# Gate products of the recurrence on half the rows of TensorE, and the decay squared on ScalarE, in a hybrid decoder layer

## The chip, the cores and the metric

One core of a Trainium2 chip runs the whole layer as one program. The metric is the device time of one execution in microseconds (us). A profiled execution also has a span, from its first to its last instruction. The engines are TensorE (PE, its weight loads shown as PEld), VectorE (DVE), ScalarE (ACT), GpSimd (POOL) and SyncE (SP), which issues the DMAs here. A time of any table or row is counted from the start of the span.

## What is computed

The layer normalises x, projects it by w_in, runs a recurrence (RG-LRU) on 512 channels beside latent attention with 8 heads, joins both through w_out, and ends with a SwiGLU FFN and a gated per-layer embedding. 1024 positions, width 1024, all in float32. The change lies in the recurrence, whose two gates r and i are block-diagonal products: 8 blocks of 64 channels, each with a 64x64 matrix of its own.

```python
xc = causal_depthwise_conv(x_rnn, conv_w, conv_b)
xb = xc.reshape(B, S, RNN_BLOCKS, RNN_BW)          # 8 blocks of 64
r = sigmoid(einsum('bsnc,ncd->bsnd', xb, w_a) + b_a).reshape(B, S, D_RNN)
i = sigmoid(einsum('bsnc,ncd->bsnd', xb, w_x) + b_x).reshape(B, S, D_RNN)
log_a = -LRU_C * r * softplus(-lru_L)
a = exp(log_a)
mult = sqrt(-expm1(2.0 * log_a))
bterm = mult * (i * xc)
_, h = associative_scan(_lin_rec_combine, (a, bterm), axis=1)
return h * gelu(x_gate)
```

## The kernel before

All activations lie transposed: channels on the 128 partitions, the 1024 positions along the row, worked in two halves of 512 (`HS`). Each float32 product is made of three products of rounded parts (fp32r): high weights with the high and the low part of the data, and low weights with the high part (names ending in `_h` and `_l`). Function `mm` issues these three for both halves, each half into a PSUM bank of its own. PSUM is handed out as four single banks (`bank`) and two double ones (`wide`). The banks of a pair are named `_a` and `_b`, by `pair`.

The stages follow each other: the latent and key projection (`g1`), then ten column tiles of w_in (`wn`: two latent query tiles, four tiles r0 to r3 of the recurrence, four gate tiles g0 to g3), of which one half goes into pairs of banks (`wn_a`, `wn_b`) and the other into wide ones (`wn`). For a tile r the convolution makes `xc` and its two parts (`rg_front`, L794). After two such tiles `rg_pair` (L802) is put in: per tile and gate a 128x128 weight matrix whose diagonal holds the two 64x64 blocks and which is zero elsewhere (`_layout`, L1529 to L1534), six products into `rg_a` and `rg_b` (the two halves of the positions), and two sigmoids of 128x512 that read the banks (L813). Then the decay: `rg_t` by Tanh, `rg_r` by Exp, its square on VectorE into `xc` (L822), the root of the term before the input, and the scan. Among this work stand the keys (`kr`, `kps`), the values (`v`), the queries (`qps`), then eight heads of scores (`s`), transposes (`tp`) and weighted sums (`av`), the output projection (`wo`), and the FFN, whose products (`ff_z`, `ff_y`, `ff_x`) are made by Strassen-Winograd's scheme with seven products in place of eight.

The order of all of this is not the order of the code. Every call is recorded in a `Plan` (L141) as an operation with a cost and with what it depends on. `Plan.order` (L244) then plays a clock: at each step it looks for each engine through the operations that are ready, takes the one with the lowest key for which its PSUM banks and SBUF slots are free (L289), charges the cost that `cost` (L167) gives it, and moves on. POOL operations, and VectorE operations with two inputs in SBUF or a fast copy form, are marked as using a shared port (`shares`, L197); one that is taken while the port is in use starts when it comes free (L318 to L320), and its engine stands until then. ScalarE's activation tables count 1.28 us a switch. All instructions are recorded in one helper, so that every row of the profile has the line of `emit` (L372), and instructions are told apart by their tiles. `emit` issues them in the planned order, each engine in its own sequence.

Of the kernel before, what the change touches and what calls it, by code (L numbers as in the profile page):

```python
# [16 lines left out]
P = 128  # L17
S = 1024
D = 1024
HB = 512  # L20
# [120 lines left out]
class Plan:  # L141
# [25 lines left out]
    def cost(self, eng, fn, a, k, out):  # L167
        w = out.width() if isinstance(out, View) else 0
        if fn == "dma_start":
            v = k["out"] if isinstance(k["out"], View) else k["in_"]  # L170
            return v.shape[0] * v.width() * 4 / 360e3, 2.1
        if eng == "tensor":
            if fn == "transpose":
                return 0.108, 0.18
            return max(w * 0.000417 + 0.0135, 0.113), 0.18
        if eng == "vector":
            if fn == "reciprocal":
                return 0.065 + w * 0.0063, 0.13
            if fn == "tensor_tensor_scan":
                return 0.068 + w * 0.0021, 0.13  # L180
            if fn in ("tensor_reduce", "reduce_sum"):
                return 0.065 + k["in_"].width() * 0.00104, 0.13
            ptr = 0.061 * any(isinstance(x, View) for x in (k.get("scalar"), *a[2:])) if fn == "scalar_tensor_tensor" else 0.0
            one = fn in ("tensor_copy", "tensor_scalar", "tensor_scalar_mul", "tensor_scalar_add", "tensor_scalar_max")
            if one and all(v.buf.tag not in PS for v in [*a, *k.values()] if isinstance(v, View)):
                return 0.068 + w * 0.00052, 0.13
            return 0.068 + ptr + w * 0.00104, 0.13
        if eng == "scalar":
            src = k["in_"] if "in_" in k else a[1]
            c = (0.052 if src.buf.tag in PS else 0.093) + w * 0.000833  # L190
            c += 0.093 * sum(isinstance(k.get(n), View) for n in ("scale", "bias"))
            c += 0.2 * isinstance(k.get("accum_out"), View)
            return c, 0.14
        return 0.15 + w * (0.0033 if fn == "tensor_copy" else 0.0022), 0.14
# [49 lines left out]
    def order(self):  # L244
# [28 lines left out]
        while left:  # L273
            while frees and frees[0][0] <= t:
                _, _, tag, n = heapq.heappop(frees)
                free[tag] += n
            moved = False
            for e in names:
                while future[e] and future[e][0][0] <= t:
                    _, i, o = heapq.heappop(future[e])  # L280
                    heapq.heappush(avail[e], (o.key, i, o))
                if busy[e] > t or not avail[e]:
                    continue
                pick, skipped, best = None, [], None
                tries = 0
                while avail[e] and tries < 40:
                    i, _, o = heapq.heappop(avail[e])
                    tries += 1
                    ok = all(b.placed or free[b.tag] > min(unplaced(b), RES.get(b.tag, 99)) for b in o.bufs)  # L289
                    if ok:  # L290
                        key = i
                        if e == "scalar" and o.table and o.table not in SAME.get(table, ()):
                            key = i + SWITCH
                        if best is None or key < best[0]:
                            if best is not None:
                                skipped.append((best[1], best[2].idx, best[2]))
                            best = (key, i, o)
                        else:
                            skipped.append((i, o.idx, o))
                        if e != "scalar" or key == i:  # L300
                            break
                    else:
                        skipped.append((i, o.idx, o))
                for s in skipped:
                    heapq.heappush(avail[e], s)
                if best is None:
                    continue

                soon = next((r for r, _, x in future[e][:6] if r < t + HOLD and r + 0.05 < t + best[2].cost
                             and x.cost < 0.25 and x.key + 20 < best[0]), None) if e != "tensor" else None  # L310
                if soon is not None:
                    heapq.heappush(avail[e], (best[1], best[2].idx, best[2]))
                    continue
                o = best[2]
                moved = True
                start = t
                c = o.cost
                if o.port:  # L318
                    start = max(t, port)
                    port = start + c  # L320
                if o.table and o.table not in SAME.get(table, ()):
                    table = FIRST[o.table]
                    c += 1.28
                for b in o.bufs:
                    if b.placed:
                        continue
                    b.placed = True
                    free[b.tag] -= 1
                    q, d = queue[b.tag], ahead[b.tag]
                    d[b.pos] = True  # L330
                    while head[b.tag] < len(q) and d[head[b.tag]]:
                        head[b.tag] += 1
                busy[e] = start + c
                o.end = start + c + o.lat
                o.st = start
                out.append((t, o.idx, o))
                left -= 1
                for b in o.bufs:
                    b.left -= 1
                    b.done = max(getattr(b, "done", 0.0), start + c + LAT[e, "tensor"] if b.tag in PS and e != "tensor" else o.end)  # L340
                    if not b.left:
                        heapq.heappush(frees, (b.done, b.pos, b.tag, 1))
                for s in o.succ:
                    s.npred -= 1
                    r = start + c + (LAT[e, s.eng] if (e, s.eng) in LAT else o.lat)
                    s.ready = max(s.ready, r)
                    if not s.npred:
                        heapq.heappush(future[s.eng], (s.ready, s.idx, s))
            nxt = [busy[e] for e in names if busy[e] > t and (avail[e] or future[e])]
            nxt += [future[e][0][0] for e in names if future[e] and future[e][0][0] > t]  # L350
            if frees:
                nxt.append(frees[0][0])
            nxt = [x for x in nxt if x > t]
            if not left:
                break
            if not nxt:
                raise RuntimeError("the plan does not fit")
            t = min(nxt)
# [21 lines left out]
XLATE = 100  # L380
HOLD = 0.15
KLATE = 100
WARM = 9
NV0 = 4
TL = 300
# [14 lines left out]
def hybrid_layer(ctx, tc, xT, pT, pos, vec, const, const2, w1, wn, wrg, wq, wkv, wo, wg, wu, *rest):  # L400
# [114 lines left out]


    order = [(("w1", k), w1[k], 192) for k in range(8)] + [(("wn", i), wn[i], S) for i in range(2)]
    order += [(("rg", 0), wrg, S)] + [(("wn", i), wn[i], S) for i in range(2, 10)]
    order += [(("wkv", 0), wkv, S), (("wq", 0), wq[0], S)]
    order += [(("wq", 1), wq[1], S)]  # L520
    order += [(("wo", n), wo[n], S) for n in NO]
# [280 lines left out]
    def rg_pair(js):  # L802
        yield
        gs = {}
        for j in js:
            xc, x2 = fronts[j]
            r, i = slot("rg_r"), slot("rg_i")
            for t, (dst, b) in enumerate(((r, "b_a"), (i, "b_x"))):
                pss = pair("rg")
                c = slice((2 * j + t) * P, (2 * j + t + 1) * P)  # L810
                mm(pss, rgw[0][:, c], rgw[1][:, c], x2, True, True)
                for h in range(2):
                    A.activation(dst[:, HS[h]], pss[h], AF.Sigmoid, bias=col(b, j))  # L813
            G.tensor_mul(i, i, xc)
            gs[j] = [r, i, xc]
        for j in js:
            r, i, xc = gs[j]
            th = slot("rg_t")
            gs[j].append(th)
            A.activation(th, r, AF.Tanh, scale=cpos[:, j:j + 1])  # L820
            A.activation(r, r, AF.Exp, scale=cneg[:, j:j + 1])
            V.tensor_mul(xc, r, r)  # L822
            V.scalar_tensor_tensor(out=th, in0=xc, scalar=1.0, in1=th, op0=ALU.add, op1=ALU.mult)
        for j in js:
            A.activation(gs[j][3], gs[j][3], AF.Sqrt)
# [663 lines left out]
def _layout(a):  # L1489
# [36 lines left out]

    starts = [1024, 1152] + [(0 if s[0] == "r" else 512) + int(s[1]) * P for s in IN_ORDER]
    o["wn"] = c(np.stack([ntile(w, np.r_[s:s + P]) for s in starts]))
    rg = np.zeros((P, 8, P), np.float32)  # L1529
    for j in range(4):  # L1530
        for t, nm in enumerate(("w_rg_a", "w_rg_x")):
            for b in range(2):
                rg[b * 64:(b + 1) * 64, 2 * j + t, b * 64:(b + 1) * 64] = a[nm][0, 2 * j + b]
    o["wrg"] = rg.reshape(P, 8 * P)  # L1534
    w = a["w_q_up"][0]
    qs = []
    for h in range(NH):
# [44 lines left out]
```

## Time and profile before

| what | value |
| --- | --- |
| median of 3 runs | 1178.99 us (1178.84 to 1179.36) |
| the profiled execution | 1179.9 us, span 1178.1 us |
| TensorE busy | 1158.5 us, 98% of the span, 5601 products |
| VectorE, ScalarE, POOL busy | 980.8, 639.0, 182.2 us |
| mean granted clock of TensorE | 0.995 |
| moved by DMA | 155.64 MB, mean 132 GB/s |

The profile is read from the whole to the part. Busy time of a product is modelled and overlaps that of the next, so how tightly TensorE works is better seen from the distance between the starts of two products than from their durations. A row of the timeline gives start, duration, engine, operation, tiles, shapes, and in brackets the idle time of the engine before it, with what ended it.

### The profile page before, as it was taken

The page shows a single profiled execution, that of the slowest core. Times are in us where ns is not written, and L with a number is a line of the kernel's source. Part 1 is how long each engine was busy: PE and PEld are TensorE (multiplying, and loading weights), DVE is VectorE, ACT ScalarE, POOL GpSimd, SP SyncE. Part 2 cuts the span into 40 slices and gives each one's busy share as a digit, 9 for nine tenths or more (in the row PEclk, how much of TensorE's full clock was granted, in tenths as well). Part 3 has the DMA queues.
Part 4 walks back from the last instruction along what each step waited for, and adds up shares of the span by engine and source line. Part 5 has one row for each costly group of instructions (what it writes and reads, how often), then busy time and mean ns, then how long its engine had stood idle before and what let it go on. Part 6 is the DMA issues. An engine that isn't in the chain of part 4 may idle for free.

```text
span 1178.1 us, 15370 instructions
## 1 busy us (share of the span) xinstructions
PE 1158.5 (98%) x5601; PEld 962.7 (82%) x5601; DVE 980.8 (83%) x1509; ACT 639.0 (54%) x1077; POOL 182.2 (15%) x114
## 2 busy tenths in 40 slices
PE   9999999999999999999999999999999999999996
PEld 6888888888888888888888888888787888888895
DVE  7999888888978598878988897868997658787986
ACT  8457968877946364545444454435332224465664
POOL 0002140421100032233313331233000000000000
PEclk9999999999999999999999999999999999999998
DMA  9001100000405134334442454357877764032342
GB/s 338 19 18 36 36 1 1 1 1 1 161 4 203 65 135 168 141 110 179 176 157 105 152 196 160 117 206 254 335 254 284 264 245 161 26 140 76 125 162 72
DMA packets 47675, 155.64 MB, mean 132 GB/s; under 512 B 5360, under 2 KB 8688, under 8 KB 47600
## 3 DMA queue, kind: packets, MB, share of 16 engines
q1 hardware_dynamic: 47056, 154.14, 35.9%
q8 instruction: 44, 0.72, 0.3%
q10 hardware_dynamic: 544, 0.52, 0.1%
q14 instruction: 31, 0.25, 0.1%
HBM read 109.56 MB, written 45.09 MB: 131 GB/s over the span
## 4 chain that ended last, share of the span: by engine, by line
PE 87%; DVE 5%; ACT 4%; DMA 3%; issue 1%; SPq 0%; DVEq 0%; ACTq 0%
PE ff_z L372 28%; PE ff_y L372 14%; PE ff_x L372 7%; PE wo L372 6%; PE plg L372 5%; PE s L372 4%; PE wn L372 4%; PE av L372 3%; PE tp L372 2%; PE wn_b L372 2%; PE wn_a L372 2%; PE qps L372 1%; PE g L372 1%; DMA wd_r<-in_wd 1%; PE wo_a L372 1%; PE wo_b L372 1%
## 5 line engine op out<-in xcount | busy, mean ns | idle before, releaser
L372 POOL TENSOR_TENSOR silu<-silu,nf_rb 128x512 f32<-128x512 f32 x77 | 122.4, 1613 | 393.1 <-DVE silu L372 235.9
L372 PE MATMUL ff_z<-hx,wd 128*128 128x512 f32 x528 | 128.2, 390 | 1.5 <-ACT wd L372 0.9
L372 PE MATMUL ff_z<-x,wg 128*128 128x512 f32 x528 | 127.6, 390 | 0.0
L372 PE MATMUL ff_z<-x,wu 128*128 128x512 f32 x528 | 127.0, 389 | 0.0
L372 PEld LDWEIGHTS ff_z<-hx,wd 128*128 128x128 f32 x528 | 98.6, 188 | 23.5 <-DVE h L372 1.5
L372 PEld LDWEIGHTS ff_z<-x,wu 128*128 128x128 f32 x528 | 99.1, 188 | 20.6
L372 PEld LDWEIGHTS ff_z<-x,wg 128*128 128x128 f32 x528 | 98.9, 188 | 20.7 <-ACT silu L372 0.3
L372 ACT ACTIVATE hx<-silu 128x512 fp32r<-128x512 f32 x55 | 34.6, 629 | 72.6 <-DVE silu L372 43.1
L372 ACT ACTIVATE wd<-wd_r 128x256 fp32r<-128x256 f32 (+2 forms) x64 | 30.4, 492 | 70.0 <-DMA wd_r<-in_wd 31.4
L372 PE MATMUL ff_y<-hx,wd 128*128 128x512 f32 x264 | 65.3, 390 | 0.0
L372 PE MATMUL ff_y<-x,wg 128*128 128x512 f32 x264 | 64.1, 390 | 0.0
L372 PE MATMUL ff_y<-x,wu 128*128 128x512 f32 x264 | 63.4, 389 | 0.0
L372 PE MATMUL plg<-hg_h,wpg_h 128*128 128x256 f32 (+1 forms) x192 | 61.6, 321 | 1.2 <-ACT wpg_h L372 0.9
L372 PE MATMUL plg<-hg_l,wpg_h 128*128 128x256 f32 (+1 forms) x192 | 61.3, 319 | 0.0
L372 PE MATMUL plg<-hg_h,wpg_l 128*128 128x256 f32 (+1 forms) x192 | 60.9, 318 | 0.0
L372 DVE TENSOR_TENSOR h<-ff_z,h 128x512 f32<-128x512 f32 x64 | 44.2, 692 | 18.9 <-PE ff_z L372 18.8
L372 PEld LDWEIGHTS ff_y<-hx,wd 128*128 128x128 f32 x264 | 49.5, 188 | 10.7 <-DVE wd L372 0.4
L372 PEld LDWEIGHTS ff_y<-x,wu 128*128 128x128 f32 x264 | 49.5, 188 | 10.3
L372 PEld LDWEIGHTS ff_y<-x,wg 128*128 128x128 f32 x264 | 49.4, 188 | 10.3 <-ACT x L372 0.2
L372 DVE TENSOR_REDUCE nm<-s 128x1 f32<-128x128 f32 (+3 forms) x64 | 48.2, 753 | 10.4 <-PE s L372 9.9
L372 POOL TENSOR_TENSOR o<-h,no_rb 128x256 f32<-128x256 f32 x2 | 1.4, 730 | 351.1 <-ACT no_rb L372 351.1
L372 ACT ACTIVATE silu<-silu 128x512 f32<-128x512 f32 x44 | 27.7, 633 | 48.5 <-POOL silu L372 47.2
(411 smaller groups left out, 2979.6 us busy)
## 6 DMA issues: line engine op xcount, KB each, us to landing
hx<-hx SPq DMA_DIRECT2D x140, 512.0 KB, 3.7
wg_r<-in_wg SPq DMA_DIRECT2D x22, 512.0 KB, 5.3
wu_r<-in_wu SPq DMA_DIRECT2D x22, 512.0 KB, 3.4
wpg_raw<-in_wpg SPq DMA_DIRECT2D x20, 512.0 KB, 3.5
wn_raw<-in_wn SPq DMA_DIRECT2D x10, 512.0 KB, 7.2
wo_raw<-in_wo SPq DMA_DIRECT2D x8, 512.0 KB, 4.6
h<-in_xT SPq DMA_DIRECT2D x8, 512.0 KB, 5.0
hd<-h SPq DMA_DIRECT2D x8, 512.0 KB, 3.4
```

The lines of the kernel that those rows point to most:

```text
L372: getattr(self.engines[o.eng], o.fn)(*a, **k)
```

## The change

The weights of the two gates of a 128-channel tile are laid side by side in one 128x128 block: rows 0 to 63 hold the first 64-channel block's matrices, rows 64 to 127 the second's, with the gates in opposite column order for the two. A product takes 64 rows of weights and 64 rows of data at `tile_position` (0, 0) or (64, 0), and its result has both gates of one block on 128 partitions. `rg_a` and `rg_b` are now the two blocks, for one half of the positions at a time. Four sigmoids of 64x512 read each pair of banks, two of them from other partitions than they write to. The gate weights take 512 columns instead of 1024. The square of the decay is made by ScalarE.

The planner gets two new rules: a product with 64 rows of weights is charged half the cost, and a VectorE operation that needs the shared port isn't taken while the port stays in use for more than 0.3 us (`PORT`); another operation may go before it. Since the planner orders all engines by these costs, the order changes beyond the gates too.

```diff
--- before.py
+++ after.py
@@ -172,7 +172,9 @@
         if eng == "tensor":
             if fn == "transpose":
                 return 0.108, 0.18
-            return max(w * 0.000417 + 0.0135, 0.113), 0.18
+            c = max(w * 0.000417 + 0.0135, 0.113)
+
+            return c / 2 if k["lhsT"].shape[0] == 64 else c, 0.18
         if eng == "vector":
             if fn == "reciprocal":
                 return 0.065 + w * 0.0063, 0.13
@@ -286,7 +288,7 @@
                 while avail[e] and tries < 40:
                     i, _, o = heapq.heappop(avail[e])
                     tries += 1
-                    ok = all(b.placed or free[b.tag] > min(unplaced(b), RES.get(b.tag, 99)) for b in o.bufs)
+                    ok = not (e == "vector" and o.port and port > t + PORT) and all(b.placed or free[b.tag] > min(unplaced(b), RES.get(b.tag, 99)) for b in o.bufs)
                     if ok:
                         key = i
                         if e == "scalar" and o.table and o.table not in SAME.get(table, ()):
@@ -350,6 +352,7 @@
             nxt += [future[e][0][0] for e in names if future[e] and future[e][0][0] > t]
             if frees:
                 nxt.append(frees[0][0])
+            nxt.append(port - PORT)
             nxt = [x for x in nxt if x > t]
             if not left:
                 break
@@ -380,6 +383,7 @@
 XLATE = 100
 HOLD = 0.15
 KLATE = 100
+PORT = 0.3
 WARM = 9
 NV0 = 4
 TL = 300
@@ -515,7 +519,7 @@
 
 
     order = [(("w1", k), w1[k], 192) for k in range(8)] + [(("wn", i), wn[i], S) for i in range(2)]
-    order += [(("rg", 0), wrg, S)] + [(("wn", i), wn[i], S) for i in range(2, 10)]
+    order += [(("rg", 0), wrg, HB)] + [(("wn", i), wn[i], S) for i in range(2, 10)]
     order += [(("wkv", 0), wkv, S), (("wq", 0), wq[0], S)]
     order += [(("wq", 1), wq[1], S)]
     order += [(("wo", n), wo[n], S) for n in NO]
@@ -805,12 +809,20 @@
         for j in js:
             xc, x2 = fronts[j]
             r, i = slot("rg_r"), slot("rg_i")
-            for t, (dst, b) in enumerate(((r, "b_a"), (i, "b_x"))):
+
+            c = slice(j * P, (j + 1) * P)
+            for h in range(2):
                 pss = pair("rg")
-                c = slice((2 * j + t) * P, (2 * j + t + 1) * P)
-                mm(pss, rgw[0][:, c], rgw[1][:, c], x2, True, True)
-                for h in range(2):
-                    A.activation(dst[:, HS[h]], pss[h], AF.Sigmoid, bias=col(b, j))
+                for n, (w, x) in enumerate(((0, 0), (0, 1), (1, 0))):
+                    for b in range(2):
+                        rows = slice(64 * b, 64 * b + 64)
+                        T.matmul(pss[b], lhsT=rgw[w][rows, c], rhs=x2[x][rows, HS[h]], start=n == 0, stop=n == 2,
+                                 tile_position=(64 * b, 0))
+                for b in range(2):
+                    for t, (dst, nm) in enumerate(((r, "b_a"), (i, "b_x"))):
+                        ch = slice(64 * b, 64 * b + 64)
+                        rows = slice(64 * (t ^ b), 64 * (t ^ b) + 64)
+                        A.activation(dst[ch, HS[h]], pss[b][rows], AF.Sigmoid, bias=col(nm, j)[ch])
             G.tensor_mul(i, i, xc)
             gs[j] = [r, i, xc]
         for j in js:
@@ -819,7 +831,7 @@
             gs[j].append(th)
             A.activation(th, r, AF.Tanh, scale=cpos[:, j:j + 1])
             A.activation(r, r, AF.Exp, scale=cneg[:, j:j + 1])
-            V.tensor_mul(xc, r, r)
+            A.activation(xc, r, AF.Square)
             V.scalar_tensor_tensor(out=th, in0=xc, scalar=1.0, in1=th, op0=ALU.add, op1=ALU.mult)
         for j in js:
             A.activation(gs[j][3], gs[j][3], AF.Sqrt)
@@ -1526,12 +1538,12 @@
 
     starts = [1024, 1152] + [(0 if s[0] == "r" else 512) + int(s[1]) * P for s in IN_ORDER]
     o["wn"] = c(np.stack([ntile(w, np.r_[s:s + P]) for s in starts]))
-    rg = np.zeros((P, 8, P), np.float32)
+    rg = np.empty((P, 4, P), np.float32)
     for j in range(4):
         for t, nm in enumerate(("w_rg_a", "w_rg_x")):
             for b in range(2):
-                rg[b * 64:(b + 1) * 64, 2 * j + t, b * 64:(b + 1) * 64] = a[nm][0, 2 * j + b]
-    o["wrg"] = rg.reshape(P, 8 * P)
+                rg[b * 64:(b + 1) * 64, j, (t ^ b) * 64:(t ^ b) * 64 + 64] = a[nm][0, 2 * j + b]
+    o["wrg"] = rg.reshape(P, 4 * P)
     w = a["w_q_up"][0]
     qs = []
     for h in range(NH):
```

## Rows read from the trace of the kernel before

**Rows 1.** Page, part 1: busy us, share of span, number of instructions by engine.
```profile
PE 1158.5 (98%) x5601; PEld 962.7 (82%) x5601; DVE 980.8 (83%) x1509; ACT 639.0 (54%) x1077; POOL 182.2 (15%) x114
```

**Rows 2.** Page, part 2: TensorE's granted clock in 40 slices, tenths of full.
```profile
PEclk9999999999999999999999999999999999999998
```

**Rows 3.** Table by stage: busy us (instructions) per engine, clock, DMA share, GB/s.
```profile
84.00:164.50 80.50, 80.07 (x357) 66.12 (x357) 69.68 (x80) 63.19 (x76) 19.30 (x8) 1.00 0.08 27
164.50:320.00 155.50, 154.03 (x946) 128.04 (x945) 131.19 (x224) 126.70 (x275) 35.53 (x22) 1.00 0.07 24
350.00:1050.00 700.00, 698.49 (x3083) 576.17 (x3083) 575.92 (x863) 307.70 (x526) 122.35 (x77) 1.00 0.48 178
```

**Rows 4.** Timeline at the first gate products: start us, us, engine, what.
```profile
86.78 0.39 PE L372 MATMUL rg_a<-xc_h,rg_h 128*128 128x512 f32 x1
86.78 0.19 PEld L372 LDWEIGHTS rg_b<-xc_h,rg_h 128*128 128x128 f32 x1
87.00 0.39 PE L372 MATMUL rg_b<-xc_h,rg_h 128*128 128x512 f32 x1
```

**Rows 5.** TensorE's waits from 84 to 1050 us: total us, times, longest.
```profile
PE ff_z L372 <- ACT wd L372: 0.9, 1, 0.9
...
PE qps L372 <- DVE pt L372: 0.2, 1, 0.2
```

**Rows 6.** Timeline of TensorE around one transpose, and four in a row.
```profile
168.63 0.39 PE L372 MATMUL qps<-cq_l,wq_h 128*128 128x512 f32 x1
168.86 0.27 PE L372 MATMUL tp<-cs,pA 128*128 128x128 f32 x1
168.88 0.47 PE L372 MATMUL s<-k_h,q_h 128*128 128x512 f32 x1
169.20 0.39 PE L372 MATMUL s<-k_l,q_h 128*128 128x512 f32 x1
...
171.31 0.60 PE L372 MATMUL tp<-cs,pA 128*128 128x128 f32 x4
```

**Rows 7.** Timeline of TensorE at the one visible wait of the gates' stretch.
```profile
133.24 0.39 PE L372 MATMUL wn_a<-x_h,wn_h 128*128 128x512 f32 x1
134.06 0.47 PE L372 MATMUL wn_b<-x_h,wn_h 128*128 128x512 f32 x1 [0.43 <-DVE k_l L372]
```

**Rows 8.** ScalarE, 84 to 165 us: busy us, mean ns, idle us before them.
```profile
L372 ACT ACT_TABLE_LOAD x10 | 12.8, 1283 | 0.2
L372 ACT ACTIVATE v<-v 128x512 fp32r<-128x512 f32 x8 | 4.5, 591 | 6.3 <-PE v L372 6.2
L372 ACT ACTIVATE sq<-rg_h 128x1024 f32<-128x1024 f32 x3 | 3.2, 1058 | 0.6 <-DVE rg_h L372 0.6
L372 ACT ACTIVATE k_h<-kr 64x512 fp32r<-64x512 f32 x6 | 3.1, 590 | 0.8 <-DVE k_l L372 0.8
```

**Rows 9.** Timeline of ScalarE at four places.
```profile
90.91 0.68 ACT L372 ACTIVATE rg_i<-rg_a,vc 128x512 f32<-128x512 f32 x1
91.48 0.68 ACT L372 ACTIVATE rg_i<-rg_b,vc 128x512 f32<-128x512 f32 x1
...
115.31 0.69 ACT L372 ACTIVATE rg_r<-rg_a,vc 128x512 f32<-128x512 f32 x1 [4.76 <-PE rg_a L372]
...
153.63 0.60 ACT L372 ACTIVATE v<-v 128x512 fp32r<-128x512 f32 x1 [5.56 <-PE v L372]
```

**Rows 10.** Timelines of VectorE and POOL, and VectorE's squares from 84 to 165 us.
```profile
97.77 2.00 DVE L372 TENSOR_TENSOR wn_l<-wn_raw,wn_h 128x1024 fp32r<-128x1024 f32 x1 [1.35 <-ACT wn_h L372]
...
95.83 2.86 POOL L372 TENSOR_TENSOR rg_i<-rg_i,xc 128x1024 f32<-128x1024 f32 x1 [0.49 <-ACT rg_i L372]
...
117.14 1.22 DVE L372 TENSOR_TENSOR wn_l<-wn_raw,wn_h 128x1024 fp32r<-128x1024 f32 x1
...
L372 DVE TENSOR_TENSOR xc<-rg_r 128x1024 f32<-128x1024 f32 x4 | 4.8, 1222 | 2.6 <-POOL rg_i L372 2.3 <-ACT rg_r L372 0.3
```

## The prediction

> **What bounds the kernel now.** I read the page's busy shares first, then its slices, then a table by stage, then the waits of TensorE, and only then single instructions. TensorE is busy for 98% of the span [rows 1] and holds the full clock in all slices but the last [rows 2]. The table by stage [rows 3] shows where the change lies: the gates are worked between 84 and 164.5 us, where TensorE is busy 80.07 of 80.50 us; the heads follow until 320 us and the FFN runs from 350 to 1050. Busy is a modelled figure, so the check is the pace: in the gates' own rows one 128x512 product starts 0.22 to 0.23 us after the last [rows 4], and 357 products in 80.5 us are 0.2255 us each. There is hardly a free slot here. The weight load (0.19 us) runs beside the product before it, so it costs nothing now. Between 84 and 1050 us, TensorE's waits that the trace can name are eight, from 0.9 down to 0.2 us, 3.3 us together [rows 5]. So time can fall in two ways only: fewer slots on TensorE, or some of these 3.3 us.
>
> **The change part by part.**
>
> *The products.* Before, each gate of each 128-channel tile is three products a half, so 4 x 2 x 3 x 2 = 48. After, there are also 48: two blocks, three products, two halves, four tiles. Each streams the same 512 columns from 64 rows of operands. Nothing is saved by one such product alone; the saving needs an upper-half product beside a lower-half one, and for that the two must stand next to each other. The order on TensorE at the first two tiles, where rg_a is the block in rows 0 to 63 and rg_b the block in rows 64 to 127, before:
>
> ```order
> L372 MATMUL wn_b<-x_h,wn_l 128x512
> L372 MATMUL rg_a<-xc_h,rg_h 128x512
> L372 MATMUL rg_b<-xc_h,rg_h 128x512
> L372 MATMUL rg_a<-xc_l,rg_h 128x512
> L372 MATMUL rg_b<-xc_l,rg_h 128x512
> L372 MATMUL rg_a<-xc_h,rg_l 128x512
> L372 MATMUL rg_b<-xc_h,rg_l 128x512
> L372 MATMUL wn<-x_h,wn_h 128x512 x2
> L372 MATMUL wn<-x_l,wn_h 128x512
> L372 MATMUL rg_a<-xc_h,rg_h 128x512
> L372 MATMUL rg_a<-xc_l,rg_h 128x512
> L372 MATMUL rg_a<-xc_h,rg_l 128x512
> ```
> (there a and b are only the two halves of the sequence), and after:
>
> ```order
> L375 MATMUL rg_b<-xc_h,rg_l 128x512
> L375 MATMUL wn<-x_h,wn_h 128x512 x2
> L375 MATMUL wn<-x_l,wn_h 128x512
> L375 MATMUL wn<-x_h,wn_l 128x512 x2
> L375 MATMUL rg_a<-xc_h,rg_h 128x512
> L375 MATMUL rg_a<-xc_l,rg_h 128x512
> L375 MATMUL rg_a<-xc_h,rg_l 128x512
> L375 MATMUL wn<-x_h,wn_h 128x512
> L375 MATMUL rg_b<-xc_h,rg_h 128x512
> L375 MATMUL rg_b<-xc_l,rg_h 128x512
> L375 MATMUL rg_b<-xc_h,rg_l 128x512
> L375 MATMUL wn<-x_h,wn_h 128x512
> ```
> The first half of a pair of tiles still alternates a and b; everything else comes as three products of one block, then full-height wn products, then three of the other. Over the whole list the 48 products form 14 runs: 2 runs alternate (6 pairs), 12 are threes of one block. The threes have no partner, so 36 products keep their 0.226 us: no gain, and none is possible, since the neighbours use all rows. The 6 pairs save between 0 and one slot each: 6 x 0.226 = 1.36 us. I take the full 1.36, because in a pair both the rows of the array and the PSUM banks are separate.
>
> *Going in and out of half height.* 14 runs are 28 changes between a product of all rows and one of half the rows. The trace has no such change. The nearest row is another change of TensorE's kind of work: a 128-column transpose among 512-column products [rows 6]. From 168.63 to 169.20 us stand two products and one transpose: 0.57 us, less 2 x 0.226 is 0.118, of four transposes in a row (0.60 us, one alone 0.27) each further one adds 0.11; so a change to and back costs about 0.01. I take 0.01 each: 28 x 0.01 = 0.3 us. The lower end is 0, since a change can't do away with columns. The upper end is the part of a product that now lies beside the next one: 0.39 us long, next one after 0.226, so 0.163 [rows 4]; 28 x 0.163 = 4.6 us. If the next weight load is held up as well, 0.19 more: 28 x 0.351 = 9.8 us.
>
> *A wait that goes.* The one visible wait in the stretch is wn_b for VectorE's k_l: 134.06 less 133.24 is 0.82 where 0.226 is the pace, so 0.59 us lost [rows 7]. In the order before, the two rope-key products stand together and wn_a and wn_b then need two banks almost at once; after, the two stand four wn products apart, and all 24 of wn_a come before wn_b:
>
> ```order
> L372 MATMUL kps<-ckv_h,wkv_l 128x512
> L372 MATMUL wn_a<-x_h,wn_h 128x512
> L372 MATMUL wn_a<-x_l,wn_h 128x512
> L372 MATMUL wn_a<-x_h,wn_l 128x512
> L372 MATMUL wn_a<-x_h,wn_h 128x512
> L372 MATMUL wn_b<-x_h,wn_h 128x512
> L372 MATMUL wn_b<-x_l,wn_h 128x512
> ```
> and, on the same engine at the same place, after:
>
> ```order
> L375 MATMUL wn_a<-x_h,wn_l 128x512
> L375 MATMUL kps<-ckv_h,wkv_h 128x512
> L375 MATMUL kps<-ckv_l,wkv_h 128x512
> L375 MATMUL kps<-ckv_h,wkv_l 128x512
> L375 MATMUL wn<-x_h,wn_l 128x512
> L375 MATMUL wn<-x_h,wn_h 128x512 x2
> L375 MATMUL wn<-x_l,wn_h 128x512 x2
> L375 MATMUL wn_b<-x_h,wn_h 128x512
> ```
> I count the 0.59 as saved; what is late next is in the following part.
>
> *ScalarE.* The sigmoids go from 16 of 128x512 to 32 of 64x512:
>
> ```order
> L372 ACTIVATE rg_r<-rg_a,vc 128x512
> L372 ACTIVATE xc<-zr,vc 128x1024
> L372 ACTIVATE rg_r<-rg_b,vc 128x512
> L372 ACTIVATE rg_i<-rg_a,vc 128x512
> L372 ACTIVATE rg_i<-rg_b,vc 128x512
> ```
> becomes
>
> ```order
> L375 ACTIVATE rg_r<-rg_a,vc 64x512
> L375 ACTIVATE xc<-zr,vc 128x1024
> L375 ACTIVATE rg_i<-rg_a,vc 64x512
> L375 ACTIVATE rg_r<-rg_b,vc 64x512
> L375 ACTIVATE rg_i<-rg_b,vc 64x512
> L375 ACTIVATE rg_r<-rg_a,vc 64x512
> ```
> Half the partitions don't halve the time: a 64x512 copy out of PSUM takes 590 ns, a 128x512 one 591 [rows 8]. Two sigmoids start 0.57 us apart [rows 9], so 16 more are +9.1 us. The four squares come to ScalarE at the 1.06 us of its sq rows: +4.2. The order after has 8 table loads from the gates to the first Exp of the scores where before has 10: -2 x 1.28 = -2.6. Sum: +10.8 us. ScalarE is idle for 80.50 - 63.19 = 17.3 us of this stretch [rows 3], the largest pieces 4.76 us (waiting for rg_a) and 5.56 us (for v) [rows 9]. TensorE covers ScalarE's delay as long as it has wn products to put between; the new order does that. I take 0; the upper end is below. A gain is excluded, for ScalarE gets no lighter.
>
> *VectorE, POOL and the DMAs.* VectorE loses four products of 1.22 us, 4.9 us, and is waited for little here: 0. The planner's rule on the shared port changes VectorE's order where POOL works. What it avoids is seen in one row: wn_l took 2.00 us at 97.77 while POOL worked from 95.83 to 98.69, and 1.22 at 117.14 [rows 10]. In the FFN, where POOL does most, VectorE's freed time is hidden behind TensorE, which waits there 1.5 us of 700 [rows 3]: 0, with those 1.5 us as the most it can give, and as much as it can cost if a swapped pair comes late. The gate weights shrink from 512 to 256 KB, loaded long before use: 0.
>
> **Sum.** -1.36 + 0.3 - 0.59 = -1.65 us against the profiled execution's 1179.9 us (span 1178.1 and 1.8 around it), which lies 0.9 above the median 1179.0. So 1177.3 us. What a measurement can tell from no change is 0.2%, 2.4 us, so faster means below 1176.6.
>
> **The rivals.**
>
> *Every change of height empties the array (slower).* 28 x 0.163 = 4.6 in place of 0.3: 1179.0 - 1.36 - 0.59 + 4.6 = 1181.6; with weight loads uncovered 1186.9. It turns the sum to a loss from 0.07 us a change and to slower from 0.154. For it: the tail of 0.163 exists. Against it: the transposes pay nothing. The Trainium skill, page "TensorEngine Tiling (Array Packing)", section "Tiling Modes", Key Properties, says that changing the tiling mode drains the engine, though not changing the tile alone; no run here shows one yet. By it, this rival's first figure would hold.
>
> *ScalarE comes late to the first scores (slower).* If neither of the two long idle pieces can be filled, 17.3 - 4.76 - 5.56 = 7.0 us of room meet 10.8 of work: the first Exp is 3.8 us late and TensorE, which holds only two wide score tiles, stops: 1177.3 + 3.8 = 1181.1. It decides once more than 6.5 us of the idle can't be used. Against it: v and kps are moved forward, which fills the 5.56.
>
> *More waits go (faster).* Of the other 2.9 us of waits in the heads and the FFN, half or all go with the new order: 1177.3 - 1.5 to - 2.9, so 1174.4 to 1175.8. For it: VectorE has 4.9 us less to do just before the heads.
>
> *The halves don't run together.* 0 instead of 1.36: 1178.7, the change not doing what it says. The page "TensorE: Matmul & The Clock Gate", Part 3, says products in different row groups overlap with starts about 4 ns apart; by that it would be 1177.3 as summed.
>
> **How the numbers follow.** The sum as it stands 0.37 (its own range 1176 to 1179, a third of it below 1176.6); more waits go 0.24; halves not together 0.14; drains 0.17; ScalarE late 0.08. Faster: 0.24 + 0.12 = 0.36. Slower: nearly all of 0.25, 0.24. Same: 0.40. The range reaches down to 1174 and up to 1183.5, which leaves out the drain with uncovered loads.
>
> **What would show it.** In the trace after: rg_a and rg_b starting nearly together in 2 runs and 0.226 apart in 12; the distance from the last rg product to the next wn (0.23 if changes are free, 0.39 if they drain, 0.58 with the load); the 32 sigmoids 0.57 apart; no wait of wn_b near 133; the first Exp of the scores near 164 us. The forecast is wrong if changes cost over 0.154 us, if ScalarE has no idle left before 164 us and TensorE waits for it, or if the heads' rhythm moves by more than 2 us.

## The result: slower by 0.9%

| | before | after |
|---|---|---|
| median of 3 runs (lowest to highest) | 1178.99 us (1178.84 to 1179.36) | 1189.96 us (1189.04 to 1190.13) |
| profiled execution: span | 1178.1 us | 1187.2 us |
| ratio to before, 95% interval | | 1.0086 [1.0072, 1.0101] |
| first Exp of the attention scores starts | 165.77 us | 175.83 us |

The forecast was 1177.3 with a range of 1174.0 to 1183.5; the time is outside it and on the other side. The last line of the table is the shortest account: the change sits between 84 and 165 us, and the heads' first Exp comes 10.06 us late; the profiled span is 9.1 us longer.

**By stage.** The table by stage of the changed kernel (the same three stretches as [rows 3], same columns):

```profile
84.00:164.50 80.50, 78.76 (x326) 57.43 (x325) 55.16 (x61) 70.44 (x85) 11.96 (x5) 1.00 0.08 27
164.50:320.00 155.50, 151.10 (x920) 125.39 (x919) 130.07 (x224) 122.77 (x267) 39.45 (x24) 1.00 0.05 15
350.00:1050.00 700.00, 698.78 (x3080) 575.40 (x3079) 570.66 (x862) 306.41 (x526) 121.89 (x77) 1.00 0.48 176
```

Against [rows 3], TensorE gets through 326 products in the gates' 80.5 us where it did 357, and 920 rather than 946 in the heads. The FFN keeps its pace (3080 and 3083). TensorE's busy time hides most of the first loss: 78.76 of 80.50 us still looks full. ScalarE's busy time in the gates rises from 63.19 to 70.44 us.

**TensorE at the first gate products.** The timeline that answers [rows 4] (start us, length us, engine, line, what):

```profile
86.29 0.39 PE L375 MATMUL wn_a<-x_h,wn_l 128*128 128x512 f32 x1
86.52 0.39 PE L375 MATMUL wn_b<-x_h,wn_l 128*128 128x512 f32 x1
86.83 0.49 PE L375 MATMUL rg_a<-xc_h,rg_h 64*128 64x512 f32 x1
86.84 0.49 PE L375 MATMUL rg_b<-xc_h,rg_h 64*128 64x512 f32 x1
87.17 0.39 PE L375 MATMUL rg_a<-xc_l,rg_h 64*128 64x512 f32 x1
87.17 0.39 PE L375 MATMUL rg_b<-xc_l,rg_h 64*128 64x512 f32 x1
87.40 0.39 PE L375 MATMUL rg_a<-xc_h,rg_l 64*128 64x512 f32 x1
87.41 0.39 PE L375 MATMUL rg_b<-xc_h,rg_l 64*128 64x512 f32 x1
87.73 0.73 PE L375 MATMUL wn<-x_h,wn_h 128*128 128x512 f32 x2
...
89.88 0.39 PE L375 MATMUL rg_a<-xc_h,rg_l 64*128 64x512 f32 x1
90.21 0.49 PE L375 MATMUL wn<-x_h,wn_h 128*128 128x512 f32 x1
90.63 0.49 PE L375 MATMUL rg_b<-xc_h,rg_h 64*128 64x512 f32 x1
90.97 0.39 PE L375 MATMUL rg_b<-xc_l,rg_h 64*128 64x512 f32 x1
```

Two things are read from the starts. The halves do run together: rg_a and rg_b start 0.00 to 0.01 us apart, so a pair takes one slot. And each change of height is paid for twice. From the last wn to the first rg it is 86.83 - 86.52 = 0.31 us instead of 0.226, and from that pair to the next 87.17 - 86.84 = 0.33 instead of 0.23. On the way out the same: 87.73 - 87.41 = 0.32, and the first wn after a run is longer too (0.49 in the row at 90.21, where a wn between its like has 0.39). About 0.1 before and 0.1 behind, 0.2 us a change. The single wn between two threes shows both ends of it: from 90.21 to 90.63 is 0.42 us for one product.

**ScalarE.** The timeline of the sigmoids, which answers [rows 9]:

```profile
90.46 0.69 ACT L375 ACTIVATE rg_i<-rg_a,vc 64x512 f32<-64x512 f32 x1
91.17 0.69 ACT L375 ACTIVATE rg_r<-rg_b,vc 64x512 f32<-64x512 f32 x1
91.87 0.68 ACT L375 ACTIVATE rg_i<-rg_b,vc 64x512 f32<-64x512 f32 x1
92.58 0.68 ACT L375 ACTIVATE rg_r<-rg_a,vc 64x512 f32<-64x512 f32 x1
```

A sigmoid of half the partitions lasts as long as one of all (0.68 to 0.69 us), as forecast, but the next one starts 0.70 us later and not 0.57. So the 32 take 32 x 0.70 = 22.4 us where the 16 took 16 x 0.57 = 9.1: +13.3, not +9.1. The last of them shows the delay, before and after:

```profile
126.31 0.70 ACT L372 ACTIVATE rg_i<-rg_b,vc 128x512 f32<-128x512 f32 x1
```
```profile
132.99 0.68 ACT L375 ACTIVATE rg_i<-rg_b,vc 64x512 f32<-64x512 f32 x1
```

It starts 6.7 us later; Tanh, Exp and the squares of the last tiles stand behind it on ScalarE.

**Where TensorE waits now.** Its waits from 84 to 200 us (engine, tile, line, whom it waits for: us in total, times, longest):

```profile
PE qps L375 <- DVE qf L375: 2.2, 1, 2.2
PE v L375 <- DVE k_l L375: 1.6, 1, 1.6
PE v L375 <- DVE v L375: 0.9, 1, 0.9
PE tp L375 <- DVE k_l L375: 0.6, 1, 0.6
PE tp L375 <- DVE ya L375: 0.3, 1, 0.3
```

With one more of 0.2 they are 5.8 us; before, the waits of the same stretch were 1.3 us. The releaser named is VectorE each time, but VectorE is not short of time: it is busy for 55.16 of the 80.5 us. Its timeline shows why it is late:

```profile
136.16 1.23 DVE L375 TENSOR_TENSOR zg<-wn,nx_rb 128x1024 f32<-128x1024 f32 x1 [10.79 <-PE wn L375]
...
144.37 2.36 DVE L375 SCALAR_TENSOR_TENSOR rg_t<-xc,rg_t 128x1024 f32<-128x1024 f32 x2 [2.10 <-ACT xc L375]
...
151.27 2.35 DVE L375 TENSOR_TENSOR rg_i<-rg_i,rg_t 128x1024 f32<-128x1024 f32 x2
153.54 4.47 DVE L375 TENSOR_TENSOR_SCAN rg_h<-rg_r,rg_i 128x1024 f32<-128x1024 f32 x2
157.92 2.33 DVE L375 TENSOR_TENSOR rg_h<-rg_h,zg 128x1024 f32<-128x1024 f32 x2
160.17 1.22 DVE L375 TENSOR_TENSOR wq_l<-wq_raw,wq_h 128x1024 fp32r<-128x1024 f32 x1
161.31 1.38 DVE L375 TENSOR_TENSOR k_l<-kps,k_h 64x512 fp32r<-64x512 f32 x2
```

VectorE stood idle for 10.79 us until TensorE's wn was there, then 2.10 us for ScalarE's xc, and the whole chain behind the gates' last tiles (gate product, scan, rg_h) came late. The two scans run from 153.54; before, the later of the two started at 145.39:

```profile
145.39 2.28 DVE L372 TENSOR_TENSOR_SCAN rg_h<-rg_r,rg_i 128x1024 f32<-128x1024 f32 x1
```

The last k_l, whose k_h ScalarE began at 152.52, needs nothing of that chain but stands behind it in VectorE's order and starts at 161.31. TensorE had run out of wn products by then and waited for it. The wait of wn_b near 133 us [rows 7] is gone, as forecast.

### The profile page after: what moved, and what is told of

It reads as the page before. It is cut to its first block, busy times and chain, and to the rows that moved or that the text cites. A ratio compares the mean times of both kernels' runs of the same rounds, so it can differ in the third digit from the quotient of the medians.

```text
span 1187.2 us, 15393 instructions
## 1 busy us (share of the span) xinstructions
PE 1164.5 (98%) x5601; PEld 959.2 (81%) x5601; DVE 967.6 (82%) x1505; ACT 652.2 (55%) x1095; POOL 178.4 (15%) x114
## 4 chain that ended last, share of the span: by engine, by line
PE 85%; DVE 6%; ACT 3%; DMA 2%; issue 1%; POOL 1%; SPq 0%; DVEq 0%; ACTq 0%; POOLq 0%
PE ff_z L375 28%; PE ff_y L375 14%; PE ff_x L375 7%; PE wo L375 6%; PE plg L375 5%; PE s L375 4%; PE wn L375 4%; PE av L375 3%; PE tp L375 3%; PE wn_a L375 2%; PE wn_b L375 2%; PE qps L375 2%; PE g L375 1%; DMA wd_r<-in_wd 1%; DVE h L375 1%
```

## The experiments

Three theories stand in the expectations. **A**: the changes of TensorE's height cost about 0.2 us each, some 4.3 us after what the pairs save. **B**, from r5 on **S**: ScalarE's and VectorE's chain comes late whatever the products cost, and by S it is the split sigmoids that load it. **C**, from r5 on **P**: the planner wrote a bad order, by its port rule (C) or because it charges a 64-row product half a slot (P). In r9 two readings of the 0.70 us stand against each other: a sigmoid of 64 partitions is slow to follow (**L**), or the change from one half of the partitions to the other costs (**D**). Ratios are to the kernel before on the same chip, whose medians there were 1178.3 to 1179.1 us, with 95% intervals. "Changes" counts TensorE's changes of height in the order as built.

| run | changes | time added by the gates' sigmoids, us | median us | ratio | first Exp, later than 165.77 by |
|---|---|---|---|---|---|
| after | 28 | 13.3 | 1189.96 | 1.0086 [1.0072, 1.0101] | 10.1 |
| r1 full height | 0 | 13.3 | 1185.70 | 1.0056 [1.0041, 1.0071] | 5.2 |
| r2 no port rule | 28 | 13.3 | 1190.18 | 1.0099 [1.0083, 1.0116] | 11.2 |
| r3 square back | 28 | 13.3 | 1190.87 | 1.0101 [1.0086, 1.0116] | 12.7 |
| r4 gates back | 0 | 0 | 1179.65 | 1.0010 [1.0000, 1.0019] | 1.2 |
| r5 full cost | 24 | 13.3 | 1187.38 | 1.0069 [1.0054, 1.0084] | 6.3 |
| r6 full height and cost | 0 | 13.3 | 1186.01 | 1.0061 [1.0046, 1.0077] | 6.0 |
| r7 split sigmoids alone | 0 | 13.3 | 1189.50 | 1.0094 [1.0077, 1.0111] | 10.5 |
| r8 grouped | 16 | 13.3 | 1186.29 | 1.0059 [1.0043, 1.0075] | 5.9 |
| r9 split, by half | 0 | 11.4 | 1184.70 | 1.0049 [1.0036, 1.0062] | 5.2 |
| r10 whole sigmoids | 26 | 0 | 1184.58 | 1.0051 [1.0038, 1.0063] | 4.5 |
| r11 grouped, whole | 12 | 0 | 1180.07 | 1.0008 [0.9999, 1.0016] | 1.6 |
| r12 grouped, sigmoids charged | 16 | 13.3 | 1184.68 | 1.0052 [1.0038, 1.0066] | 5.2 |
| r13 8 sigmoids repeated | 0 | 4.6 | 1182.25 | 1.0024 [1.0012, 1.0035] | 2.9 |
| r14 24 repeated | 0 | 13.7 | 1188.06 | 1.0084 [1.0067, 1.0102] | 8.7 |
| r15 as r11, square on VectorE | 14 | 0 | 1178.83 | 0.9995 [0.9986, 1.0003] | -0.3 |

The added times are counts by measured distances: 32 x 0.70 - 16 x 0.57, in r9 16 x 0.70 + 16 x 0.585 - 9.1, in r13 and r14 8 and 24 x 0.57.

**r1: the same order, over all rows.** The weights are padded with zeros to all 128 rows and every product reads all of x; all engines keep their order.

```diff
-T.matmul(pss[b], lhsT=rgw[w][rows, c], rhs=x2[x][rows, HS[h]], ..., tile_position=(64 * b, 0))
+T.matmul(pss[b], lhsT=rgw[w][:, cb], rhs=x2[x][:, HS[h]], ...)
```

> The changed kernel with the same order on all engines, instruction for instruction, but each gate product over all 128 rows (the other block's rows of the weights are zero, so the result is the same). Theory A, the 28 changes of height cost about 0.2 us each and the 6 pairs give back 1.36: TensorE's own time falls by 4.4 us and the kernel to about 1185.5. Theory B, VectorE's and ScalarE's chain to k_l and qf (TensorE waits 5 us for it between 161 and 171 us) sets the end of the stretch whatever the products cost: it stays within 1.5 us of 1190. Rival C, the planner's new order alone costs the time: no change.

1185.70 us: theory A's figure (1185.5). The timeline at the same place:

```profile
86.42 0.39 PE L377 MATMUL wn_b<-x_h,wn_l 128*128 128x512 f32 x1
86.65 0.39 PE L377 MATMUL rg_a<-xc_h,rgw_h 128*128 128x512 f32 x1
86.87 0.39 PE L377 MATMUL rg_b<-xc_h,rgw_h 128*128 128x512 f32 x1
...
90.05 0.39 PE L377 MATMUL wn<-x_h,wn_h 128*128 128x512 f32 x1
90.27 0.39 PE L377 MATMUL rg_b<-xc_h,rgw_h 128*128 128x512 f32 x1
```

With the same neighbours and no change of height the pace is 0.22 to 0.23 us everywhere. The changed kernel is 1189.96 - 1185.70 = 4.3 us slower than this; 28 x 0.2 - 1.36 is 4.2. The rest, 6.6 us over before, is untouched, and so are the waits for qf and k_l (2.2 and 1.6 us, as in the changed kernel).

**r2, r3, r4: the other two edits.** r2 drops the port rule, r3 puts the square back on VectorE, r4 is the kernel before with those two edits alone.

```diff
-ok = not (e == "vector" and o.port and port > t + PORT) and all(...)
+ok = all(...)
```
```diff
-A.activation(xc, r, AF.Square)
+V.tensor_mul(xc, r, r)
```

> The changed kernel without the planner's port rule. A and B: within 2 us of 1190, because the products and the sigmoids are as before. C, the port rule's order is what puts k_l late: 1180 to 1186, and the waits of v and qps for VectorE near 161 to 171 us are gone.

> The changed kernel with the decay squared on VectorE again: 4.2 us off ScalarE, 4.9 us onto VectorE. A: within 2 us of 1190. B, if ScalarE's load is what makes the chain late: 2 to 4 us faster, 1186 to 1188. If VectorE's load is what makes it late: slower, 1191 to 1194.

> The kernel before with two of the three edits, the decay squared on ScalarE and the port rule; the gate products and sigmoids as before. A and B (the gates' products or their sigmoids cost the time): 1177 to 1181. C, the order by the port rule or the square: 1184 or more.

Neither r2 nor r3 is faster than the changed kernel, and r4 is 0.0 to 0.19% slower than before. Port rule and square together cost about 1 us (0 to 2.2); the products and sigmoids cost the rest. Theory C's port rule is out.

**r5, r6: the planner's charge.** r5 charges a 64-row product a full slot; r6 does so in r1.

```diff
-return c / 2 if k["lhsT"].shape[0] == 64 else c, 0.18
+return c, 0.18
```

> The changed kernel, but the planner charges a 64-row product a full slot again, as the trace shows it outside of pairs. Theory P, the order was made for gates that TensorE would do in half the time, and VectorE's k_l and qf stand in it behind work that comes later than planned: the 4.9 us of waits of v and qps go, 1184 to 1186. Theory S, the 32 sigmoids (0.70 us apart, 13 us more on ScalarE) make the chain late whatever the order: 1188.5 to 1191.

> The run with full-height products (1185.7) with the planner charging a full slot for each. P: 1179 to 1181.5, since nothing but the sigmoids is then left of the change and the order fits them. S: 1184 to 1186.5, the sigmoids' load being as before.

r5 lies between the two forecasts. It is some 2 us faster than the changed kernel, by intervals that still overlap, and has 24 changes and 10 pairs: 24 x 0.2 - 10 x 0.226 = 2.5 us against 4.2 gives 1.7 of it. r6 is no faster than r1, as S had it. So a right charge helps as far as it brings half-height products together, and P isn't where the 6.6 us are.

**r7: the split sigmoids alone,** in the kernel before.

```diff
-A.activation(dst[:, HS[h]], pss[h], AF.Sigmoid, bias=col(b, j))
+for e in range(2):
+    ch = slice(64 * e, 64 * e + 64)
+    A.activation(dst[ch, HS[h]], pss[h][ch], AF.Sigmoid, bias=col(b, j)[ch])
```

> The kernel before with one edit: each sigmoid of 128x512 split into two of 64 partitions, which the planner knows of (it charges the split ones 0.57 each). S: 3 to 6 us slower than before, 1182 to 1185. P: 1178 to 1180.5, as ScalarE has 17.3 us idle in the stretch. The trace also tells whether two that stay on their own partitions start 0.57 or 0.70 us apart.

1189.50: the split alone costs as much as the whole change, more than S expected (1182 to 1185). In this order TensorE also waits 3.0 us for VectorE's zg, which no other run has at that size, and its profile shows two stretches at the lower clock, some 3 us together (last section). The sigmoids here read and write the same partitions and still stand 0.70 us apart, so it isn't the move from one half to the other between input and output.

**r8: the six products of a half issued together,** so that all alternate: 8 runs, 24 pairs, 16 changes.

```diff
-for n, (w, x) in enumerate(((0, 0), (0, 1), (1, 0))): ... T.matmul(pss[b], ...)
+T.halves(out=pss[0], accum_out=pss[1], w0=rgw[0][:, c], ...)   # one entry of the plan, 1.08 us
```

> The changed kernel with the six products of one half of a tile recorded as one operation, so that they always stand together, upper and lower half in turn: 8 runs, 16 changes, 24 pairs, charged 1.08 us a run in the plan. TensorE: 24 slots of 0.226 saved, 5.4 us, and 16 x 0.2 = 3.2 us for the changes: 2.2 us less than before, 6.6 less than the changed kernel. With P the waits go too: 1176.5 to 1179.5. With S they stay: 1181 to 1184.

Here TensorE's own account is better than before the change (16 x 0.2 - 24 x 0.226 = -2.2 us), and the time is 7 us worse, above both forecasts. Part of the account isn't kept: in three of the eight runs the first pair starts 0.17 to 0.57 us apart, 1.1 us in all, and twice it is a sigmoid that rg_b's engine waits for (0.5 us); and behind a wait of 2.17 us some 1.5 us go to the lower clock. Beside the 1 us of r4 that leaves the sigmoids.

**r9: does the split cost, or the switching between halves?** r7 with the two sigmoids of the same partitions one behind the other.

```diff
-for h in range(2):
-    for e in range(2):
+for e in range(2):
+    for h in range(2):
```

> The kernel before with each sigmoid of the gates split into two of 64 partitions, ordered so that two with the same partitions and the same bias follow each other (all columns of one half of the partitions, then of the other). Theory L (a sigmoid of 64 partitions is itself slower to follow than one of 128): all stand 0.70 us apart as where the halves alternated, and the time stays at 1188 to 1191. Theory D (it is the change of partitions that costs some 0.13 us): the second of each two stands 0.57 us behind the first, 16 x 0.13 = 2.1 us of ScalarE's time go, and the time is 1184 to 1188.

Theory D holds. ScalarE's timeline:

```profile
90.56 0.68 ACT L372 ACTIVATE rg_r<-rg_a,vc 64x512 f32<-64x512 f32 x1
91.15 0.67 ACT L372 ACTIVATE rg_r<-rg_b,vc 64x512 f32<-64x512 f32 x1
91.85 0.68 ACT L372 ACTIVATE rg_i<-rg_a,vc 64x512 f32<-64x512 f32 x1
92.43 0.67 ACT L372 ACTIVATE rg_i<-rg_b,vc 64x512 f32<-64x512 f32 x1
```

90.56 to 91.15, on the same half, is 0.59; 91.15 to 91.85, from one half to the other, is 0.70; 91.85 to 92.43, on one half again, 0.58. In the kernel before, two sigmoids with different biases on the same partitions stood 0.57 apart (this row, and the first of [rows 9] at 90.91), so it isn't the bias:

```profile
90.34 0.67 ACT L372 ACTIVATE rg_r<-rg_b,vc 128x512 f32<-128x512 f32 x1
```

The time is 4.8 us below r7's, more than ScalarE's 2 us; TensorE's wait for zg is 0.9 here where r7 had 3.0, and one stretch at the lower clock is in the profile where r7 has two.

**r10: the changed kernel with whole sigmoids.** Each product's result is taken over all 128 partitions, which mixes the two gates, so the output isn't the layer's (r11 and r15 do the same).

```diff
-for b in range(2):
-    for t, (dst, nm) in enumerate(((r, "b_a"), (i, "b_x"))):
-        ...
-        A.activation(dst[ch, HS[h]], pss[b][rows], AF.Sigmoid, bias=col(nm, j)[ch])
+for t, (dst, nm) in enumerate(((r, "b_a"), (i, "b_x"))):
+    A.activation(dst[:, HS[h]], pss[t], AF.Sigmoid, bias=col(nm, j))
```

> The changed kernel with its products as they are, but sigmoids over all 128 partitions of each product's result, as before the change (this mixes the two gates, so the output is not the reference's). If the cause is the two parts found so far, only TensorE's changes of height are left: 1178.5 + 4.4 = 1183, between 1182 and 1184.5, and the waits for VectorE's query and key halves are gone. If the order of the changed plan or the pairs themselves cost more than that, it stays at 1186 or above.

1184.58 is just above the range: 6.0 us over before by the ratio, of which 26 changes less 9 pairs make 5.2 - 2.0 = 3.2 and the other two edits (r4) about 1. The waits for qf are gone. Some 1.8 us are left, little more than the interval's 1.5 to either side; 1.1 of it is what TensorE waits more than before from 84 to 200 us (2.4 against 1.3), and what makes these waits isn't shown.

**r11 and r15: grouped, with whole sigmoids;** r15 has the square on VectorE.

> The kernel with the six products of a half issued together (16 changes of height, 24 pairs) and sigmoids over all 128 partitions (this mixes the two gates, so the output is not the reference's). If both parts of the cause are sized right: 16 x 0.2 - 24 x 0.226 = -2.2 us against before, 1176 to 1177.5, and the first scores' exponential at about 166 us as before. If something else of the change costs, 1178.5 or above.

> The grouped kernel with sigmoids over all 128 partitions (mixes the two gates, so the output is not the reference's), and the square on VectorE as before the change. If ScalarE's 4.2 us of squares took the gain of the pairs there: 1175.5 to 1177.5. If not (the plan's order, or TensorE's waits for VectorE): 1178.5 to 1180.5, as with the square on ScalarE.

Both miss the gain that the account gives them. r11 is level with before; r15 is at most 0.14% faster. Its TensorE has -2.6 us to its credit (14 changes, 24 pairs), of which about 0.6 shows. Its waits:

```profile
PE s L385 <- ACT pB L385: 0.9, 1, 0.9
PE qps L385 <- DVE v L385: 0.5, 1, 0.5
PE tp L385 <- ACT pA L385: 0.4, 1, 0.4
```

With two more of 0.3 they are 2.4 us, 1.1 more than before's in the same stretch. So even with sigmoids that cost nothing more, these pairs gave nothing that can be measured. Between r11 and r15 the square's place is worth 1.3 us, at the edge of what the intervals separate.

**r12: r8 with the sigmoids charged 0.70 us.**

```diff
+c += 0.13 * (isinstance(k.get("bias"), View) and out.shape[0] == 64)
```

> The grouped kernel with the split sigmoids, and the planner charging each sigmoid of 64 partitions the 0.70 us that it takes rather than 0.57. If the load on ScalarE itself is what costs, a plan that knows it changes little: 1184.5 to 1187 (1186.3 without it). If it was the plan's wrong idea of ScalarE's times, most of the loss goes: 1178 to 1182.

1184.68 against 1186.29: no difference that the intervals separate, and most of the loss stays. It is the load and not the plan's wrong idea of it, though this order loses more to the clock than r8's: behind a wait of 3.15 us its products stand 0.43 us apart for about 3 us of loss.

**r13 and r14: ScalarE's time alone.** The kernel before, with sigmoids of 128 partitions issued again into the same place; the planner knows of them.

```diff
+for _ in range((2, 1)[h]):      # r14: (3, 2)[h]
     A.activation(dst[:, HS[h]], pss[h], AF.Sigmoid, bias=col(b, j))
```

> The kernel before with 8 of the 16 sigmoids of the gates issued twice (the same result again): +8 x 0.57 = 4.6 us of ScalarE's time, nothing else. By the prediction's reading (ScalarE's waits hide it) and by theory S with its 8.7 us of idle ahead of the heads: within 1 us of before, 1178 to 1179.5. If ScalarE's added time costs at every dose in the proportion seen (13.3 us for 5 to 6): 1180 to 1181.

> The kernel before with 24 more sigmoids of the gates (8 issued three times, 8 twice): +24 x 0.57 = 13.7 us of ScalarE's time, as much as splitting them added. Theory S (it is ScalarE's time, wherever it comes from): 1183 to 1185, with the first scores' exponential some 5 us later than in the kernel before and TensorE waiting for k_l, qf or v. The rival (something else of halves of 64 partitions): within 2 us of before. By the prediction (all hidden in 17.3 us of idle): no change.

4.6 us of added ScalarE time cost 2.8 us (0.6 for each), 13.7 us cost 9.9 (0.7 for each, or 0.6 without the 1.4 us that the clock took, last section). No half partitions are in it. Both runs lie above every forecast made for them (at most 1181 and 1185): there is no free 8.7 us, and the price of an added us is above the 0.4 that 5 to 6 us for 13.3 had suggested. Every one of these kernels is planned anew, so the prices hold what the new order costs as well; that this is small is suggested, not shown, by r4, r11 and r15, which are planned anew without longer sigmoids and lie within 1.2 us of before. The wait in r14 is the changed kernel's, for k_l, only larger:

```profile
155.85 0.61 PE L372 MATMUL wn<-x_h,wn_l 128*128 128x512 f32 x2
160.28 0.47 PE L372 MATMUL v<-wkv_h,ckv_h 128*128 128x512 f32 x1 [3.81 <-DVE k_l L372]
```

and the Exp is 8.7 us late, by this row and the one of before:

```profile
174.45 0.37 ACT L372 ACTIVATE pA<-s,nm 128x128 f32<-128x128 f32 x1
```
```profile
165.77 0.37 ACT L372 ACTIVATE pA<-s,nm 128x128 f32<-128x128 f32 x1
```

In the table's last column most runs lose about what their first Exp comes late (r13 2.8 and 2.9, r9 5.8 and 5.2, r14 9.9 and 8.7, r7 11.1 and 10.5): the loss is made ahead of the scores and is not given back.

## Why the prediction was wrong

**Right.** The six pairs run together (1.36 us saved); the wait of wn_b near 133 us is gone (0.59); the squares and the port rule cost nothing that matters (r4: about 1 us); the FFN keeps its pace; half the partitions don't halve a sigmoid's time.

**Going in and out of half height: 0.01 us a change, measured 0.2.** The prediction took the price from the nearest row, a transpose among products [rows 6], and put the other end at 0.163 and 0.351. The transpose reads all rows, so it was the nearest row by kind of instruction and not by what changes. 28 x 0.2 = 5.6 in place of 0.3, which is close to the rival "Every change of height empties the array" (4.6), held at 0.17. The rule that the prediction cited for it from the Trainium skill, page "TensorEngine Tiling (Array Packing)", section "Tiling Modes", is that a change of mode drains the engine. The trace agrees in that every change costs; it adds the price, half of it before and half behind the first product of the new height. That the array is emptied isn't shown: the first product of the new height starts 0.31 to 0.32 us after the last of the old, which the profile gives a length of 0.39. By the prediction's own threshold (slower from 0.154 us a change) this term alone turns the sign: 1179.0 - 1.36 - 0.59 + 5.6 = 1182.7, which is slower but still inside the range.

**ScalarE: "+10.8 us, hidden in 17.3 us of idle, 0".** This is the step that failed most, and it takes the time out of the range. The size was too small (+13.3 for the sigmoids, +15 in all, for a switch of halves costs 0.12), but r13 shows that even 4.6 us would not have been free. Two things were overlooked. The idle of 5.56 us for v [rows 9] lies behind the gates' last sigmoid (126.31 us), so added sigmoid time can fill it only by making that sigmoid late, and the 4.76 us stand between two groups of tiles, where ScalarE waits for the products that TensorE issues then. And idle time of an engine is no cover when the engine stands in the chain: xc, sigmoid, Tanh, Exp, Square, Sqrt, then VectorE's scan and rg_h, behind them in VectorE's order k_l and qf, and in the end the scores. TensorE's reserve of wn products fills the time until it runs out; in the changed kernel it does at 161 us. The rival "ScalarE late to the first scores" named the mechanism, priced it at 3.8 us and held it at 0.08; it is some 3 to 6 us in this change. r1 leaves 6.6, of which about 1 are the other two edits; the changed kernel is 4.1 (ratios) to 5.4 (medians) above r10, of which 1.1 are r10's two changes fewer and three pairs more.

**The sum.** Of the 11.0 us (10.1 by the ratio), about 4.2 are the changes of height net of the pairs (r1), 3 to 6 the split sigmoids (r1, r10), about 1 the other two edits (r4). They don't simply add: at the 0.6 to 0.7 of r13 and r14, 13.3 us alone would cost 8 to 9.6. That a TensorE that is late itself waits less for ScalarE would explain it, and is argued, not shown.

**Open.** Why r15 gets 0.6 of its 2.6 us is told by its waits only in part. No run takes the longer sigmoids off while every engine keeps the changed kernel's order, as r1 did for the products, so their share is known only from kernels planned anew. No kernel here computes the right gates with both the pairs and whole sigmoids: with both gates side by side each bank holds half of r and half of i, and that is what splits the sigmoids.

## What to carry to other kernels

Before an engine's idle time is counted as cover, ask whether the engine stands in the chain that the next stage waits for; if it does, add a dose of its work to the kernel before and measure it (here 0.6 to 0.7 us lost for each us added, at 4.6 us as at 13.7). Half-height products can pay only in pairs and in long runs: at 0.2 us a change and 0.226 us a pair, a run needs two pairs to break even, and three products of one block between full-height neighbours only lose. Even the 2.6 us that this gives r15 were not seen in its time. Count what the layout of the result does to its readers: one packed product made two half-partition sigmoids of two gates, each as dear as a whole one.

## What the runs showed of the hardware

- A product over 64 rows beside one over the other 64 starts 0.00 to 0.01 us after it (changed kernel, 86.83 to 87.41 us), with 512 columns of 4-byte operands each. The Trainium skill, page "TensorE: Matmul & The Clock Gate", Part 3, says that starts in different row groups are about 4 ns apart; the trace, which gives hundredths of a us, agrees.
- ScalarE starts the next activation 0.57 to 0.59 us behind a 512-column one on the same partitions (before, r9) and 0.67 to 0.72 us, mostly 0.70, behind one on the other half (r7, r9, changed kernel), at equal length (0.67 to 0.69).
- Behind some waits TensorE ran at its lower clock for a while. In r14, after 3.81 us of waiting, the table by stage (columns as above) gives:

```profile
156.00:160.20 4.20, 0.47 (x3) 0.04 (x1) 4.16 (x3) 0.00 (x0) 1.28 (x1) 1.00 0.00 0
160.20:164.00 3.80, 3.72 (x10) 2.94 (x11) 3.80 (x7) 2.64 (x3) 0.00 (x0) 0.60 0.00 0
```

  The granted clock is 0.60 over the 3.8 us behind the wait, a mixture of the two levels; the products from 161.1 on stand 0.43 us apart, as at 1.2 GHz, instead of 0.226. So that wait cost some 1.4 us beside its own length: seven products, 161.10 to 163.66 us, at 0.2 more. In the changed kernel the two longest waits (2.17 and 1.56 us) were followed by products at the full pace. The length of the wait doesn't decide it by itself: behind the same 2.17 to 2.18 us the products kept 0.23 us in the changed kernel and in r1 and fell to 0.43 in r8 and r9. The profiles of r2, r3, r6, r8, r9 and r14 have one such stretch ahead of the FFN, r7 has two, r12 one of about twice the length; the kernel before, the changed kernel, r1, r4, r5, r10, r11, r13 and r15 have none. So 1.4 to 1.7 us (about 3 in r7 and r12) of those runs' losses went at the lower clock, on top of the wait (estimates from the distances of 0.43 us).
